# Five tiles instead of six in a weight ring, and the token-major weights 192 bytes into them

## The chip, the cores and the metric

One Trainium2 core runs the whole layer. Its engines work side by side and wait for each other by semaphores: TensorE (PE in the profile; PEld is its weight load), VectorE (DVE), ScalarE (ACT), GpSimd (POOL) and SyncE (SP), which issues all DMAs here. The metric is the device time of one execution in microseconds (us), median of several runs.

## The reference

One decoder layer on 512 tokens of width 1024, all in float32. The parts that matter here are the projections of the normalised input `h` and what hangs on them:

```python
z = h @ w_in                                  # queries, keys, values, gates, pool inputs
q = rope(rms_norm(q, q_norm_w), pos) * SCALE
k = rope(rms_norm(kv[:, :, :, 0], k_norm_w[:, None, :]), pos)
y_pool = pool_mixer(u_pool, pool_w, pool_scale) @ w_pool_br
y_attn = nsa_attention(q, k, v, nsa_g, ...) @ w_attn_br    # compressed, selected, window
merged = merge_g[:, :, 0] * y_pool + merge_g[:, :, 1] * y_attn
x = x + merged @ w_o
x = x + conv_ffn(rms_norm(x, ffn_norm_w), ...)             # 5504 wide, gated
```

## The kernel before

Every float32 operand is held as two parts, `hi` (rounded by ScalarE) and `lo` (the rest, subtracted by VectorE or GpSimd; `split`, L92 to L103), and a product is three matmuls: high by high, low by high, high by low. TensorE is kept fed from one ring of weight buffers in SBUF (`Ring`, L148). A call loads up to 1024 columns into one of two `st` buffers by DMA, and splits them into tiles of 512 columns, tags `hi` and `lo`, six of each. A tile is written again only when every matmul that reads its last content is done.

Two kinds of projection draw on it. Feature-major ones (`fm_tile`, matmul lines L109 to L111) use the weights as the stationary operand and stream 512 tokens; a call's 1024 columns are two tiles of each part, used up one after the other by 12 matmuls each. Token-major ones (`tok_gemm`, L319 to L321; names `tg`) use the input as the stationary operand and stream 256 weight columns; a group is two calls (`tm_weights`), four tiles of each part, and since it goes through all eight slices of the input for each of four token blocks (24 matmuls a block), it holds all four tiles until its last block. There are six such groups, two for keys and values (`kv_group`) and four for queries (`q_group`), 6 x 4 x 24 = 576 matmuls.

After a token block comes a chain: ScalarE scales and squares (L293, L294), VectorE sums (L296), ScalarE takes the root (L297), VectorE and GpSimd rotate (L300 to L303), VectorE multiplies (L308, L311), TensorE transposes (`kt`, L350; `qt`, L371), and ScalarE and VectorE write keys and queries (L97/L100, L376/L377). Beside them run the pool inputs (`pool_in`, whose `lo` parts GpSimd makes), the pool's mixing (`pool_mix`, names `pl`, `plo`, L103) and the compression (`cmp_in`, `cmp_hid`, names `ct`, `hp`, L473). PSUM has two banks for `fm`, `pl` and `hp` together.

A scheduler of the language sets each engine's order when the program is built: it puts the instructions of the source in an order by its own estimate of when each can start, and knows of the tiles. So a tile fewer changes the order, too. After the projections comes attention with gate projections filled in between (`fill`), then the output projection and the feed-forward part, all fed by the same ring.

Of the kernel before, what the change touches and what calls it, by code (L numbers as in the profile page):

```python
# [12 lines left out]
F32R = mybir.dt.float32r  # L13
# [6 lines left out]
P = 128  # L20
# [40 lines left out]
TW = (0,) * 6  # L61
# [15 lines left out]
def layer(ctx: ExitStack, tc: tile.TileContext, par, masks, xT, w_kva, w_tm, w_fm, w_pl, w_pbr,  # L77
# [5 lines left out]
    def nm(s):  # L83
        cnt[0] += 1
        return f"{s}{cnt[0]}"
# [31 lines left out]
    wr = pool(ctx, "wr")  # L117
# [30 lines left out]
    class Ring:  # L148
        def __init__(self, p, half, bufs):
            self.p, self.half, self.bufs = p, half, bufs  # L150

        def __call__(self, src, w, n, eng=None, cast=None):

            st = self.p.tile([P, 1024], F32, tag="st", name=nm("st"), bufs=self.bufs[0])
            nc.sync.dma_start(st[:, :n * w], src)
            out = []
            per = self.half // w
            for i in range(0, n, per):
                m = min(per, n - i)
                hi = self.p.tile([P, self.half], F32R, tag="hi", name=nm("hi"), bufs=self.bufs[1])  # L160
                lo = self.p.tile([P, self.half], F32R, tag="lo", name=nm("lo"), bufs=self.bufs[1])
                split(hi[:, :m * w], lo[:, :m * w], st[:, i * w:(i + m) * w], eng=eng, cast=cast)
                out += [(hi[:, j * w:(j + 1) * w], lo[:, j * w:(j + 1) * w]) for j in range(m)]
            return out

    ring = Ring(wr, 512, (2, 6))


    pk = cp.tile([P, NKEEP], F32, name="pk")
# [152 lines left out]
            yield t, ps  # L322

    def tm_weights(i):
        return ring(w_tm[:, i, :1024], 256, 4, TW[i] and g) + ring(w_tm[:, i, 1024:], 256, 4, TW[i] and g)

    heads = lambda ap: ap.rearrange("p (h d) -> p h d", d=DH)

# [130 lines left out]
    def cmp_hid(i):  # L459
# [3 lines left out]
        for c in range(2):  # L463
            st = wr.tile([P, 1024], F32, tag="st", name=nm("st"), bufs=ring.bufs[0])
            nc.sync.dma_start(st, cw1[i, :, c * 1024:(c + 1) * 1024])
            for p_ in range(4):
                tag = ("hi", "lo")[p_ % 2]
                w = wr.tile([P, 2, 2, P], F32R, tag=tag, name=nm(tag), bufs=ring.bufs[1])
                split(w[:, 0], w[:, 1], st[:, 256 * p_:256 * p_ + 256].rearrange("p (b h) -> p b h", b=2),
                      eng=CW and g)  # L470
                for b in range(2):
                    q_ = 8 * c + 2 * p_ + b
                    pe.matmul(hv, X[:, q_].rearrange("p j g n -> p (j g n)"), w[:, :, b],  # L473
                              start=q_ == 0, stop=q_ == 15)
# [89 lines left out]
    at = ExitStack()  # L564
# [401 lines left out]
```

## Time and profile before

| | us |
|---|---|
| median of 3 runs (843.36 to 844.0) | 843.49 |
| the profiled execution | 842.97 |
| its span, first to last instruction | 840.9 |
| TensorE busy in the span | 817.7 (97%) |
| VectorE busy | 571.4 (68%) |
| ScalarE busy | 464.4 (55%) |
| GpSimd busy | 233.7 (28%) |

The profile is of one execution. Matmuls overlap, so how fast TensorE goes is read from one start to the next, not from the duration of one. The projections fill the span's first 182 us, attention goes to about 480, and the feed-forward part is the rest. TensorE's clock stood at its upper level but for two stretches, one from 107 to 114 us and one from 182 to 186 us.

### The profile page before, as it was taken

The page shows a single profiled execution, that of the slowest core. Times are in us where ns is not written, and L with a number is a line of the kernel's source. Part 1 is how long each engine was busy: PE and PEld are TensorE (multiplying, and loading weights), DVE is VectorE, ACT ScalarE, POOL GpSimd, SP SyncE. Part 2 cuts the span into 40 slices and gives each one's busy share as a digit, 9 for nine tenths or more (in the row PEclk, how much of TensorE's full clock was granted, in tenths as well). Part 3 has the DMA queues.
Part 4 walks back from the last instruction along what each step waited for, and adds up shares of the span by engine and source line. Part 5 has one row for each costly group of instructions (what it writes and reads, how often), then busy time and mean ns, then how long its engine had stood idle before and what let it go on. Part 6 is the DMA issues. An engine that isn't in the chain of part 4 may idle for free.

```text
span 840.9 us, 12107 instructions
## 1 busy us (share of the span) xinstructions
PE 817.7 (97%) x4291; PEld 696.8 (83%) x4291; DVE 571.4 (68%) x1194; ACT 464.4 (55%) x985; POOL 233.7 (28%) x326
## 2 busy tenths in 40 slices
PE   7999989989999999999999999999999999999998
PEld 6888878968878878788888888888888888888888
DVE  7599976778887888886565438877777777522321
ACT  6755767757787877785334436544554454322220
POOL 5696714347575655642001200000000000000000
PEclk9999989999999999999999999999999999999999
DMA  6333132330100101011443332233332333343430
GB/s 217 103 101 113 51 101 96 107 101 25 51 26 26 51 17 35 27 39 42 135 149 112 101 103 77 101 101 101 100 91 90 97 100 116 92 128 103 113 101 26
DMA packets 23116, 72.82 MB, mean 87 GB/s; under 512 B 2832, under 2 KB 3472, under 8 KB 23056
## 3 DMA queue, kind: packets, MB, share of 16 engines
q1 hardware_dynamic: 23056, 72.05, 27.5%
q8 instruction: 34, 0.56, 0.3%
q14 instruction: 26, 0.21, 0.1%
HBM read 69.94 MB, written 2.10 MB: 86 GB/s over the span
## 4 chain that ended last, share of the span: by engine, by line
PE 85%; DVE 7%; ACT 3%; DMA 2%; issue 1%; POOL 0%; SPq 0%; ACTq 0%; DVEq 0%; POOLq 0%
PE fm L109 16%; PE fm L111 16%; PE fm L110 16%; PE op L729 5%; PE dn L109 5%; PE dn L111 5%; PE dn L110 5%; PE tp L722 4%; PE ss L691 2%; PE ss L692 2%; PE tg L321 2%; PE tg L319 2%; PE tg L320 2%; DMA st<-in_w_fm 1%; PE pb L109 1%
## 5 line engine op out<-in xcount | busy, mean ns | idle before, releaser
L97 ACT ACTIVATE hi<-st 128x512 fp32r<-128x512 f32 (+3 forms) x253 | 152.2, 607 | 189.3 <-PE fm L110 89.6
L100 DVE TENSOR_TENSOR lo<-st,hi 128x512 fp32r<-128x512 f32 (+1 forms) x210 | 145.2, 695 | 100.5 <-ACT hi L97 99.2
L109 PE MATMUL fm<-h2h,hi 128*128 128x512 f32 x344 | 134.0, 389 | 0.0
L110 PE MATMUL fm<-h2l,hi 128*128 128x512 f32 x344 | 133.8, 389 | 0.0
L111 PE MATMUL fm<-h2h,lo 128*128 128x512 f32 x344 | 133.7, 389 | 0.0
L703 POOL TENSOR_TENSOR pb<-pb,sm 128x128 f32<-128x128 f32 (+3 forms) x128 | 91.8, 748 | 49.8 <-DVE sm L700 26.1
L681 ACT ACTIVATE pb<-pb,nm 128x384 f32<-128x384 f32 (+3 forms) x128 | 70.9, 555 | 16.2 <-DVE nm L680 15.4
L111 PEld LDWEIGHTS fm<-h2h,lo 128*128 128x128 f32 x344 | 64.6, 188 | 13.5
L110 PEld LDWEIGHTS fm<-h2l,hi 128*128 128x128 f32 x344 | 64.6, 188 | 13.4
L109 PEld LDWEIGHTS fm<-h2h,hi 128*128 128x128 f32 x344 | 64.6, 188 | 13.2
L109 PE MATMUL fm<-hh,hi 128*128 128x512 f32 x160 | 71.7, 448 | 0.0
L680 DVE CUSTOM_DVE_ANT_0 pb<-ss,mk 128x384 f32<-128x384 f32 (+3 forms) x128 | 58.9, 486 | 16.7 <-PE ss L692 13.2
L110 PE MATMUL dn<-gl,hi 128*128 128x512 f32 (+1 forms) x189 | 69.1, 365 | 0.0
L111 PE MATMUL dn<-gh,lo 128*128 128x512 f32 (+1 forms) x189 | 69.1, 365 | 0.0
L109 PE MATMUL dn<-gh,hi 128*128 128x512 f32 (+1 forms) x189 | 69.1, 365 | 0.0
L111 PE MATMUL fm<-hh,lo 128*128 128x512 f32 x160 | 63.4, 397 | 0.7 <-POOL lo L100 0.7
L100 DVE TENSOR_TENSOR ptl<-tp,pth 128x512 fp32r<-128x512 f32 (+1 forms) x96 | 56.6, 594 | 10.8 <-ACT pth L97 10.2
L110 PE MATMUL fm<-hl,hi 128*128 128x512 f32 x160 | 63.4, 396 | 0.0
L97 ACT ACTIVATE pth<-tp 128x512 fp32r<-128x512 f32 (+1 forms) x96 | 49.3, 517 | 22.8 <-PE tp L722 22.5
L100 POOL TENSOR_TENSOR lo<-st,hi 128x512 fp32r<-128x512 f32 x36 | 47.2, 1313 | 41.6 <-ACT hi L97 35.6
L319 PE MATMUL tg<-hi,hh 128*128 128x256 f32 x192 | 54.4, 286 | 0.0
L320 PE MATMUL tg<-hi,hl 128*128 128x256 f32 x192 | 54.4, 286 | 0.0
(256 smaller groups left out, 1815.9 us busy)
## 6 DMA issues: line engine op xcount, KB each, us to landing
st<-in_w_up SPq DMA_DIRECT2D x43, 512.0 KB, 3.5
st<-in_w_dn SPq DMA_DIRECT2D x24, 448.0 KB, 3.4
st<-in_w_fm SPq DMA_DIRECT2D x20, 512.0 KB, 3.5
st<-in_w_tm SPq DMA_DIRECT2D x12, 512.0 KB, 3.4
st<-in_w_ab SPq DMA_DIRECT2D x8, 512.0 KB, 3.5
st<-in_w_o SPq DMA_DIRECT2D x8, 512.0 KB, 3.4
x<-in_xT SPq DMA_DIRECT2D x15, 256.0 KB, 3.7
st<-in_cw SPq DMA_DIRECT2D x4, 512.0 KB, 3.5
```

Source lines behind the costliest of these rows:

```text
L97: a.activation(hi, src, AF.Copy)
L100: (eng or v).tensor_tensor(lo, src, r32(hi), ALU.subtract)
L109: pe.matmul(ps, sh, mh_, start=first and i == 0, stop=False)
L110: pe.matmul(ps, sh, ml_, start=False, stop=False)
L111: pe.matmul(ps, sl, mh_, start=False, stop=last and i == n - 1)
L319: pe.matmul(ps[:, :n], hh[k][:, tt], H, start=k == 0, stop=False)
L320: pe.matmul(ps[:, :n], hl[k][:, tt], H, start=False, stop=False)
L680: v.tensor_tensor_reduce(p_, ps, mcaus[:, S - n:], -1.0, 3e38, ALU.add, ALU.min, nm_[:, i:i + 1])
L681: a.activation(p_, p_, AF.Exp, bias=nm_[:, i:i + 1], scale=-1.0, accum_out=sm[:, i:i + 1])
L703: g.tensor_tensor(pb[:, PBASE[i]:PBASE[i] + n], pb[:, PBASE[i]:PBASE[i] + n], sm[:, i:i + 1].to_broadcast([P, n]), ALU.mult)
L722: last = pe.transpose(tp[:, n:n + P], pb[:, PBASE[i] + j * P:PBASE[i] + (j + 1) * P], ident)
L729: pe.matmul(op[:, j * P:], V2[b][j][:, G], pt_[:, TBASE[j]:TBASE[j] + w], start=b == 0 and j == 0 and part == 0, stop=False)
```

## The change

A ring tile is now 576 columns long (512 and 64 to spare), and there are five for each part instead of six. The token-major projections' weights begin 48 columns (192 bytes) into their tiles; all others begin at the start as before. The tiles of one part lie 2304 bytes apart instead of 2048, and the ring is 1536 bytes shorter, so the buffers allocated behind it move down by that much. No operation is added or removed.

```diff
+        def part(self, tag, at=0):
+            t = self.p.tile([P, self.half + 64], F32R, tag=tag, name=nm(tag), bufs=self.bufs[1])
+            return t[:, at:at + self.half]
+
-        def __call__(self, src, w, n, eng=None, cast=None):
+        def __call__(self, src, w, n, eng=None, cast=None, at=0):
...
-                hi = self.p.tile([P, self.half], F32R, tag="hi", name=nm("hi"), bufs=self.bufs[1])
-                lo = self.p.tile([P, self.half], F32R, tag="lo", name=nm("lo"), bufs=self.bufs[1])
+                hi, lo = self.part("hi", at), self.part("lo", at)
...
-    ring = Ring(wr, 512, (2, 6))
+    ring = Ring(wr, 512, (2, 5))
...
     def tm_weights(i):
-        return ring(w_tm[:, i, :1024], 256, 4, TW[i] and g) + ring(w_tm[:, i, 1024:], 256, 4, TW[i] and g)
+        return (ring(w_tm[:, i, :1024], 256, 4, TW[i] and g, at=48)
+                + ring(w_tm[:, i, 1024:], 256, 4, TW[i] and g, at=48))
...
-                w = wr.tile([P, 2, 2, P], F32R, tag=tag, name=nm(tag), bufs=ring.bufs[1])
+                w = ring.part(tag).rearrange("p (a b h) -> p a b h", a=2, b=2)
```

The order moves on all engines between 25 and 182 us and hardly after. Three places follow. The first is ScalarE's order where the first feature-major weights are split (`hi102`, `hi104`: the two halves of the first pool input's; `hi65`, `hi67`: the last of the first group's). Before:

```order
L97 ACTIVATE hi67_511<-st64_505 128x512
L97 ACTIVATE hi102_709<-st101_707 128x512
L97 ACTIVATE hi104_713<-st101_707 128x512
L197 ACT_TABLE_LOAD
L197 ACTIVATE sr36_364<-nsum35_361,eps_111 128x512
```

In the changed kernel `hi102` stands there alone, and `hi104` comes 25 rows later, in the same one free tile, when the matmuls on `hi102` are done:

```order
L301 ACT_TABLE_LOAD
L301 ACTIVATE hss42_428<-hss42_428,eps_111 128x2
L348 ACTIVATE V202_139<-tg85_611,rstd_117 128x2x64
L297 ACTIVATE h49_459<-raw2_353,rstd_117 128x128
L298 ACTIVATE h50_460<-h49_459 128x128
L301 ACTIVATE hss47_446<-hss47_446,eps_111 128x2
L97 ACTIVATE hi104_713<-st101_707 128x512
```

So the second half of the first pool input's weights has gone from before the table load to behind seven small steps of the key chain; before, those steps ended in `hi111`, the next pool input's.

The second place is TensorE's order after the compression's matmuls (`hp`), at the transposes of the second query group's third and fourth blocks (`qt283`). Before, 24 matmuls of the next query group (`tg342`, `tg350`, `tg357`) stand between the two:

```order
L473 MATMUL hp291_1605<-lo301_1645,X185_1117 128x256 x2
L371 MATMUL qt283_1555<-pk_109,qd277_1539 128x128 x2
L319 MATMUL tg342_1808<-hi333_1790,hh0_120 128x256
L320 MATMUL tg342_1808<-hi333_1790,hl0_128 128x256
L319 MATMUL tg350_1852<-hi333_1790,hh0_120 128x256
L320 MATMUL tg350_1852<-hi333_1790,hl0_128 128x256
```

Now both pairs of transposes follow each other, and the next group's matmuls come after the pool's output (`pb`):

```order
L479 MATMUL hp291_1605<-lo301_1645,X185_1117 128x256 x2
L377 MATMUL qt283_1555<-pk_109,qd277_1539 128x128 x2
L377 MATMUL qt283_1555<-pk_109,qd285_1583 128x128 x2
L457 MATMUL ct306_1664<-pk_109,dup307_1665 128x128
L457 MATMUL ct306_1664<-pk_109,dup308_1668 128x128
L457 MATMUL ct306_1664<-pk_109,dup309_1671 128x128
L486 MATMUL ht303_1654<-pk_109,hs302_1650 128x64
L109 MATMUL pb321_1716<-plo242_1377,hi317_1708 128x512
```

So nothing stands any more between the transposes that need `qd277` and those that need `qd285`.

The third place is VectorE's order around the same stretch, from the second of the pool's mixed parts (`plo244`) to the third (`plo246`), whose PSUM bank `hp` takes over. Before:

```order
L103 SCALAR_TENSOR_TENSOR plo244_1384<-pl243_1380,pk_109,plo244_1384 128x512
L311 TENSOR_TENSOR qd270_1492<-h272_1494,hrs275_1505 128x2x2x64
L100 TENSOR_TENSOR X185_1117<-ct191_1142,X185_1117 64x8x31
L100 TENSOR_TENSOR lo318_1709<-st316_1706,hi317_1708 128x512
L305 RECIPROCAL hrs282_1552<-hss281_1545 128x4
L100 TENSOR_TENSOR lo320_1713<-st316_1706,hi319_1712 128x512
L377 TENSOR_TENSOR qp196_1163<-qt230_1317,qp196_1163 64x2x256
L311 TENSOR_TENSOR qd277_1539<-h279_1541,hrs282_1552 128x2x2x64
L103 SCALAR_TENSOR_TENSOR plo246_1391<-pl245_1387,pk_109,plo246_1391 128x512
```

Now, with the two `lo` behind it:

```order
L103 SCALAR_TENSOR_TENSOR plo244_1384<-pl243_1380,pk_109,plo244_1384 128x512
L309 RECIPROCAL hrs282_1552<-hss281_1545 128x4
L315 TENSOR_TENSOR qd277_1539<-h279_1541,hrs282_1552 128x2x2x64
L383 TENSOR_TENSOR qp196_1163<-qt230_1317,qp196_1163 64x2x256
L300 TENSOR_REDUCE hss289_1589<-h287_1585 128x4
L103 SCALAR_TENSOR_TENSOR plo246_1391<-pl245_1387,pk_109,plo246_1391 128x512
```

Seven instructions stood between the two, and four do now; `qd285` comes 13 instructions after `plo246` in the changed order and 12 after it before, and among the 13 are a different choice of `lo` parts and two steps of the compression.

## Rows read from the trace of the kernel before

**Rows 1.** Page, the chain that ended last: share of the span by engine.

```profile
PE 85%; DVE 7%; ACT 3%; DMA 2%; issue 1%; POOL 0%; SPq 0%; ACTq 0%; DVEq 0%; POOLq 0%
```

**Rows 2.** Busy time by stretch; after the engines, granted clock, DMA share, GB/s.

```profile
22.00:60.00 38.00, 36.39 (x212) 31.47 (x212) 26.51 (x62) 23.85 (x60) 28.67 (x51) 1.00 0.35 108
60.00:85.00 25.00, 23.20 (x184) 22.21 (x182) 24.17 (x53) 13.30 (x37) 17.71 (x29) 1.00 0.32 99
85.00:107.00 22.00, 18.99 (x149) 17.63 (x147) 20.82 (x47) 18.20 (x47) 16.42 (x28) 1.00 0.23 72
107.00:114.00 7.00, 5.55 (x26) 5.55 (x27) 6.75 (x14) 4.98 (x11) 0.15 (x1) 0.51 0.34 90
520.00:665.00 145.00, 145.00 (x642) 120.05 (x641) 111.57 (x168) 74.68 (x112) 0.00 (x0) 1.00 0.31 98
```

**Rows 3.** Timeline of TensorE: start, us, instruction, count; the pace of 256-column matmuls.

```profile
27.27 0.28 PE L319 MATMUL tg<-hi,hh 128*128 128x256 f32 x1
...
27.99 0.28 PE L319 MATMUL tg<-hi,hh 128*128 128x256 f32 x1
...
150.04 0.41 PE L473 MATMUL hp<-hi,X 128*128 128x256 f32 x2
...
151.97 0.28 PE L319 MATMUL tg<-hi,hh 128*128 128x256 f32 x1
```

**Rows 4.** Timeline, 27 to 41 us: splitting the pool inputs' weights.

```profile
26.93 1.15 ACT L97 ACTIVATE hi<-st 128x512 fp32r<-128x512 f32 x2 [1.39 <-DMA st<-in_w_fm]
...
34.41 0.47 PE L109 MATMUL fm<-hh,hi 128*128 128x512 f32 x1
...
38.80 0.61 ACT L97 ACTIVATE hi<-st 128x512 fp32r<-128x512 f32 x1
...
39.32 0.47 ACT L297 ACTIVATE hss<-hss,eps 128x2 f32<-128x2 f32 x2
...
39.55 1.28 POOL L100 TENSOR_TENSOR lo<-st,hi 128x512 fp32r<-128x512 f32 x1 [4.80 <-PE fm L111]
...
39.80 0.40 PE L110 MATMUL fm<-hl,hi 128*128 128x512 f32 x1
...
40.88 0.50 PE L111 MATMUL fm<-hh,lo 128*128 128x512 f32 x1 [0.68 <-POOL lo L100]
```

**Rows 5.** Timeline, 103 to 115 us: the hole before the compression, and what follows it.

```profile
103.46 0.74 DVE L103 SCALAR_TENSOR_TENSOR plo<-pl,pk,plo 128x512 fp32r<-128x512 f32 x1
...
107.65 0.74 DVE L103 SCALAR_TENSOR_TENSOR plo<-pl,pk,plo 128x512 fp32r<-128x512 f32 x1
...
108.45 0.79 PE L473 MATMUL hp<-hi,X 128*128 128x256 f32 x2 [3.24 <-DVE plo L103]
...
109.04 0.63 PE L473 MATMUL hp<-lo,X 128*128 128x256 f32 x2
...
109.47 0.63 PE L473 MATMUL hp<-hi,X 128*128 128x256 f32 x2
...
113.16 0.56 PE L319 MATMUL tg<-hi,hh 128*128 128x256 f32 x1
...
113.61 0.69 DVE L100 TENSOR_TENSOR lo<-st,hi 128x512 fp32r<-128x512 f32 x1
...
114.22 0.42 DVE L311 TENSOR_TENSOR qd<-h,hrs 128x256 f32<-128x256 f32 x1
```

**Rows 6.** Timeline at 182 us: the first compressed scores' transposes.

```profile
181.89 0.90 PE L629 MATMUL scq<-pk,cst 128*128 128x128 f32 x4 [3.39 <-DVE cst L624]
```

**Rows 7.** Timeline: one kind of VectorE step, alone and beside a GpSimd addition.

```profile
41.44 0.27 DVE L303 TENSOR_TENSOR h<-h,h 128x128 f32<-128x128 f32 x1
...
44.49 1.03 POOL L402 TENSOR_TENSOR pa<-pu 128x511 f32<-128x511 f32 x1
44.59 1.08 DVE L303 TENSOR_TENSOR h<-h,h 128x128 f32<-128x128 f32 x1
```

**Rows 8.** Waits, 186 to 841 us: us in total, times, longest.

```profile
ACT hi L97 <- PE fm L110: 88.8, 74, 4.1
```

## The prediction

> **What bounds the kernel now.** I read the chain that ended last first. TensorE holds 85% of it, VectorE 7%, ScalarE 3% and DMA 2% [rows 1]: what counts is time in which TensorE stands still or goes slowly. Then busy time by stretch [rows 2]. From 520 to 665 us TensorE is busy for 145.00 of 145 us with 642 matmuls, 145/642 = 0.226 us for each of 512 columns. The projections are another matter: 36.39 of 38 us from 22 to 60, 23.20 of 25 us from 60 to 85, 18.99 of 22 us from 85 to 107, and 5.55 of 7 us from 107 to 114, there at a granted clock of 0.51, the lower level (1.2 GHz). VectorE is busy for 24.17 + 20.82 + 6.75 = 51.7 of the 54 us from 60 to 114, so what is pushed back on VectorE there stays pushed back. The DMA share is at most 0.35. Last came the timelines of the places where the order moves [rows 4 to 6], and the waits of the rest [rows 8].
>
> So the change can act in four ways: by the address, by the tiles of the attention and feed-forward parts, by the order in the projections, and by the clock.
>
> **The address.** The 576 token-major matmuls read the same 256 columns 192 bytes further on. Between two that stand six apart, start to start is (27.99 - 27.27)/6 = 0.120 us; the compression's matmuls, which have another moving operand at another address, follow at (151.97 - 150.04)/16 = 0.121 us [rows 3]. By columns, 256/512 of 0.226 is 0.113 us; what does not shrink with the columns is twice the difference, 0.014 us. The pace is the same for two tensors that lie apart, so I take 0 for the shift. The bounds are that it takes away the whole fixed part, 576 x 0.014 = 8 us, or adds as much.
>
> The Trainium skill ("TensorE: Matmul & The Clock Gate", section "Wait — 56ns, not 53.3ns?") has a matmul take N/2.4 GHz and about 2.5 ns more when warm, 109 ns for 256 columns, and names no address; if the 120 ns of the row were brought to that, an estimate of (0.120 - 0.109) x 576 = 6.3 us would be gained, and no run here shows it.
>
> **Five tiles after 182 us.** ScalarE's `hi` waits there 74 times for TensorE, 88.8 us in all, 4.1 us at the longest [rows 8]: the splits are ahead of the matmuls and wait for tiles to come free. One tile fewer makes them wait longer, and TensorE, busy throughout [rows 2], does not see it as long as a split in one free tile (0.61 us for `hi` [rows 4]) fits into the 12 x 0.226 = 2.7 us of the tile before. I take 0; bounds 0 and +2.
>
> **The order, first place (34 to 42 us).** A token-major group holds four of five tiles through its four blocks, so one is left for feature-major halves: `hi104` can only be written when the matmuls on `hi102` are done. Before, `hi102` and `hi104` are split together, two in 1.15 us at 26.93 [rows 4], and all 24 matmuls run without a stop. In the changed order only the first 12 do. They start at 34.41 [rows 4], two token-major ones later, at 34.65, and TensorE is through at 34.65 + 2.71 = 37.4. ScalarE then has `hi104` where the next input's `hi` stood, which ran at 38.80 for 0.61 us [rows 4], with about 0.2 for one more `hss` ahead of it (two took 0.47): it ends at about 39.6, and TensorE waits 2.2 us. GpSimd's `lo` takes 1.28 us [rows 4] and ends at 40.9; TensorE has two matmuls, 0.46 us, in between and waits 0.85 more. Against these 3.1 us goes the stop of before, 39.80 + 0.23 to 40.88 [rows 4], 0.85 us, as the next input's `lo` is now covered by 24 token-major matmuls. The sum is +2.3 us; bounds +0.5 (if ScalarE's table loads fall luckily) and +4.
>
> **Second place (42 to 104 us).** The keys' transposes now stand after only four matmuls of the next input and wait for the last key step behind VectorE, and the second mixed part has some three more VectorE steps ahead, of 0.3 to 0.42 us each (`qd` took 0.42 [rows 5]), 1.0 to 1.4 us. VectorE has 45.0 us of work in the 47 from 60 to 107 [rows 2], so most of a push there arrives at TensorE. I take +1.5 us; bounds 0 and +3.4.
>
> **Third place (103 to 115 us).** Before, the compression's matmuls wait for `plo246`, 3.24 us, as the granted clock falls [rows 2, 5]. From one `plo` to the next VectorE needs 4.19 us [rows 5] with seven steps in between; with four, the wait shrinks to about 1.4 us. But the work behind it is as long as it was: `qd285` comes 13 steps after `plo246` rather than 12, and ended at 114.22 + 0.42 = 114.64 [rows 5]. Before, TensorE had 24 x 0.12 = 2.9 us of token-major matmuls from 113.16 on [rows 5] to cover that; now its transposes stand next, and TensorE waits. It gets through the two pairs at about 114.64 + 0.3 = 114.9, less 0.3 to 0.4 for the shorter `lo` work among the 13, 114.5, having done what was done at 113.16 and one pair (0.2) more: +1.2 us. What the hole gives back is thus lost at the transposes. Bounds: -0.7 (if the steps ahead of `qd285` move up with the hole) and +3.5 (if none of it does and two more steps get in).
>
> **Fourth (182 us).** The scores wait 3.39 us for `cst` [rows 6], which has one score step directly ahead on VectorE in both orders. 0, bounds -1.4 and +1.4.
>
> **Clock.** The compression's matmuls from 108.45 to 109.04 and 109.47 go at (109.47 - 109.04)/2 = 0.215 us instead of 0.12 [rows 3, 5]; 16 such cost 16 x 0.095 = 1.5 us, and the rest of the stretch somewhat more. A shorter hole might leave the clock up; the new waits at 37 to 41 us might bring it down once. I take 0, bounds -2.8 and +3.4 (one more such stretch).
>
> **Sum.** 2.3 + 1.5 + 1.2 + 0 = +5.0 us. On the profiled execution's 842.97 us that makes 848.0; the median of the runs is 843.49, half a microsecond above, well inside the range.
>
> **Rivals.**
>
> *Contention, dearer.* A VectorE addition of two SBUF operands took 0.27 us by itself and 1.08 beside a GpSimd addition [rows 7], 0.81 more. The changed order moves the key chain's steps against GpSimd's `lo` and pooling steps. If three of that chain fall beside them, 3 x 0.81 = 2.4 us come on top, and if the holes then bring one more stretch at the lower clock, 1.5 to 3.4 more: 852 to 855. For it: VectorE's lack of slack. Against: GpSimd is busy beside VectorE in before as well, so steps may as well move out of its way.
>
> The Trainium skill ("SBUF — State Buffer", section "Who interferes with whom") says that a VectorE instruction with two SBUF inputs contends with a GpSimd one that reads SBUF, and here the trace agrees, 1.08 against 0.27 us [rows 7].
>
> *Covered.* The new waits only take the place of old ones: TensorE stands idle for 38 - 36.39 = 1.6, 1.8, 3.0 and 1.5 us in the stretches of [rows 2], and if it now waits for tiles where it waited for VectorE and GpSimd before, the end moves by less than 1.7 us: 843. For it: the wait for `cst` at 182 us [rows 6] can take up what is lost before it, if VectorE, not TensorE, brings the end of the projections. Against: VectorE's chains hang on TensorE's products as well.
>
> *Not slower: the shorter hole wins.* The hole before the compression falls from 3.24 us to 1.4, -1.8 us; the clock stays up there, -1.5 for the 16 matmuls and -0.4 for transposes beside them; and only half of the first place's +2.3 arrives. Together -2.5: 840.4. It decides if the second pair of transposes waits for less than about 1 us.
>
> *The address.* If the shift spares the fixed part of 0.014 us in each of 576 matmuls, 8 us, of which 3 remain after the order's +5: 840; if it adds as much, 856.
>
> **How the numbers follow.** The forecast, order with new waits in the projections, 848.0 us: 0.60; its own range from the terms, whose bounds won't all come at one end, 845 to 851.5. Contention: 0.14. Covered: 0.12. The shorter hole: 0.09. The address: 0.05. About 0.2% (1.7 us) is what a measurement of this kernel can tell from no change. Faster by more than that takes the shorter hole and half of the address case, with a small part taken off: 0.10. Within it: covered, and the lower edge of the forecast: 0.15. Slower: the rest, 0.75. For 8 in 10 the range is 843.5 to 855: at the low end it leaves out the shorter hole, the gain by address and some of "covered", at the high end hardly more than the address's loss.
>
> **What the next profile would show.** First place right: in the first pool input, a wait of about 2.2 us of the feature-major L109 matmul for `hi` at 37 to 40 us, and 0.9 for `lo`; wrong: 24 matmuls without a stop. Second: a wait of the keys' transposes longer than before, and `plo244` 1 us or more later than the rest. Third: a wait of the compression for `plo246` near 1.4 us, and one of 2 to 3.5 us at the second pair of `qt` transposes. Address: token-major matmuls at 0.120 us from start to start, with the FFN at 0.226. From the scores' first transposes (181.89 us before) to the end, the same time as before within half a microsecond. Any stretch of granted clock at 0.5 other than the two of before is the clock term. The prediction fails if the projections end within 1.7 us of where they did, or if the time after them changes by more than that.

## The result, and the profile after

The changed kernel takes 853.74 us (median of 4 runs, 853.06 to 854.5), the kernel before 843.42 (4 runs) beside it: a ratio of 1.0121 with a 95% interval of 1.0104 to 1.0139, 10.3 us more. Forecast were 848.0 us, +5.0: the direction and the range held, the size did not.

The chain that ended last holds less of TensorE than before [rows 1]:

```profile
PE 79%; DVE 9%; ACT 5%; DMA 5%; issue 2%; POOL 1%; SPq 0%; DVEq 0%; ACTq 0%; POOLq 0%
```

Busy time by stretch, with the columns of [rows 2]; the granted clock is the third number from the end:

```profile
40.00:47.00 7.00, 6.34 (x20) 4.94 (x19) 5.70 (x17) 3.00 (x10) 5.30 (x13) 0.52 0.25 78
...
112.00:115.00 3.00, 2.58 (x6) 1.49 (x6) 2.83 (x7) 1.91 (x5) 1.79 (x4) 0.50 0.54 141
115.00:122.00 7.00, 3.13 (x21) 2.54 (x22) 6.81 (x15) 4.71 (x11) 0.15 (x1) 0.99 0.37 117
122.00:125.00 3.00, 3.00 (x9) 2.16 (x10) 2.24 (x6) 2.31 (x4) 0.76 (x3) 0.50 0.49 171
...
190.50:196.50 6.00, 5.65 (x18) 4.78 (x19) 4.09 (x13) 2.65 (x9) 0.00 (x0) 0.50 0.00 0
520.00:665.00 145.00, 145.00 (x642) 120.05 (x641) 112.67 (x170) 77.27 (x116) 0.00 (x0) 1.00 0.30 97
```

The feed-forward part is the same to the matmul. But four stretches run at the lower clock (1.2 GHz) where there were two. The mean clock of the two profiled executions says the same: 0.988 over 851.1 us is 2 x 0.012 x 851.1 = 20.4 us at half speed, 0.994 over the 840.9 of before 10.1 us. TensorE is busy nearly all through these stretches.

The first place, TensorE from 34 us, answers to [rows 4]:

```profile
34.14 0.39 PE L109 MATMUL fm<-hh,hi 128*128 128x512 f32 x1
...
36.63 0.39 PE L111 MATMUL fm<-hh,lo 128*128 128x512 f32 x1
39.52 0.50 PE L109 MATMUL fm<-hh,hi 128*128 128x512 f32 x1 [2.50 <-ACT hi L97]
39.86 0.57 PE L110 MATMUL fm<-hl,hi 128*128 128x512 f32 x1
41.10 0.79 PE L111 MATMUL fm<-hh,lo 128*128 128x512 f32 x1 [0.66 <-POOL lo L100]
...
42.97 0.63 PE L109 MATMUL fm<-hh,hi 128*128 128x512 f32 x1
43.40 0.63 PE L110 MATMUL fm<-hl,hi 128*128 128x512 f32 x1
```

The two waits are there, 2.50 and 0.66 us where 2.2 and 0.85 were forecast. What follows them was not: the next matmuls start 0.43 us apart (42.97 to 43.40), at half the pace of 0.226.

The third place, TensorE from 105 to 124 us, answers to [rows 5]. Before, the first four of these query transposes and the pairs behind them stood here:

```profile
101.72 0.63 PE L371 MATMUL qt<-pk,qd 128*128 128x128 f32 x4 [0.28 <-DVE qp L377]
...
110.32 1.05 PE L371 MATMUL qt<-pk,qd 128*128 128x128 f32 x4
```

Now:

```profile
106.43 0.28 PE L325 MATMUL tg<-lo,hh 128*128 128x256 f32 x1
108.16 0.63 PE L377 MATMUL qt<-pk,qd 128*128 128x128 f32 x4 [1.46 <-DVE X L100]
109.80 0.41 PE L377 MATMUL qt<-pk,qd 128*128 128x128 f32 x2 [1.01 <-DVE qp L383]
...
111.65 0.80 PE L109 MATMUL pl<-pli,plw 128*128 128x512 f32 x1 [0.68 <-DVE plo L103]
...
115.03 0.48 PE L479 MATMUL hp<-hi,X 128*128 128x256 f32 x2 [0.45 <-DVE plo L103]
...
118.40 0.41 PE L377 MATMUL qt<-pk,qd 128*128 128x128 f32 x2 [1.24 <-DVE qp L383]
121.04 0.44 PE L377 MATMUL qt<-pk,qd 128*128 128x128 f32 x2 [2.23 <-DVE qd L315]
...
122.95 0.79 PE L109 MATMUL pb<-plo,hi 128*128 128x512 f32 x1
123.54 0.63 PE L110 MATMUL pb<-plo,hi 128*128 128x512 f32 x1
123.97 0.63 PE L111 MATMUL pb<-plo,lo 128*128 128x512 f32 x1
```

The hole ahead of the compression shrank from 3.24 us to 0.45 (1.4 was forecast), and the second pair of transposes waits 2.23 us, within the 2 to 3.5 forecast. New to me are the 1.01 us ahead of the transposes at 109.80: they stood amid the compression's matmuls before (110.32) and now stand ahead of the pool's last mixing. The first four wait 1.46 us, where they waited 0.28. VectorE is busy for 6.81 of the 7 us from 115 to 122. And the `pb` matmuls behind start 0.43 us apart again.

At the scores the wait is about as long as in [rows 6] (3.16 against 3.39 us), but 8.96 us later, and the lower clock sets in there for 6 us and more:

```profile
190.85 1.11 PE L635 MATMUL scq<-pk,cst 128*128 128x128 f32 x4 [3.16 <-DVE cst L630]
```

Up to the first four query transposes, and up to the scores' transposes, both traces hold the same number of matmuls of each name. So the loss can be read there: +6.4 us at the first (108.16 against 101.72), +9.0 at the second, +10.2 at the end of the span. What stands behind the scores' transposes, which I had said would take the same time within half a microsecond, takes 1.2 us longer.

The token-major matmuls, which had 0.120 us from start to start [rows 3], are quicker. In two stretches of six they have (24.86 - 24.18)/6 = 0.113 and (26.72 - 26.01)/6 = 0.118 us:

```profile
24.18 0.28 PE L325 MATMUL tg<-lo,hh 128*128 128x256 f32 x1
...
24.86 0.28 PE L325 MATMUL tg<-lo,hh 128*128 128x256 f32 x1
...
26.01 0.28 PE L323 MATMUL tg<-hi,hh 128*128 128x256 f32 x1
...
26.72 0.28 PE L325 MATMUL tg<-lo,hh 128*128 128x256 f32 x1
```

That would be worth about 576 x 0.004 = 2.3 us, and yet the kernel is 10.3 us slower. The experiments have to part three things: the address, the waits of the new order, and the clock behind the waits.

### The profile page after: what moved, and what is told of

Read it like the earlier page. It is cut to its first block, busy times and chain, and to the rows that moved or that the text cites. A ratio compares the mean times of both kernels' runs of the same rounds, so it can differ in the third digit from the quotient of the medians.

```text
span 851.1 us, 12165 instructions
## 1 busy us (share of the span) xinstructions
PE 821.9 (97%) x4291; PEld 698.9 (82%) x4291; DVE 569.5 (67%) x1194; ACT 465.6 (55%) x985; POOL 231.4 (27%) x326
## 4 chain that ended last, share of the span: by engine, by line
PE 79%; DVE 9%; ACT 5%; DMA 5%; issue 2%; POOL 1%; SPq 0%; DVEq 0%; ACTq 0%; POOLq 0%
PE fm L111 16%; PE fm L109 16%; PE fm L110 16%; PE op L735 5%; PE dn L111 5%; PE dn L110 5%; PE dn L109 5%; PE tp L728 4%; PE ss L697 2%; PE ss L698 2%; DMA st<-in_w_fm 2%; DMA st<-in_w_tm 1%; ACT hi L97 1%; DVE lo L100 1%; DMA st<-in_cw 1%
## 5 line engine op out<-in xcount | busy, mean ns | idle before, releaser
L100 DVE TENSOR_TENSOR lo<-st,hi 128x512 fp32r<-128x512 f32 (+1 forms) x210 | 142.5, 683 | 97.4 <-ACT hi L97 96.4
```

Source lines behind the costliest of these rows:

```text
L100: (eng or v).tensor_tensor(lo, src, r32(hi), ALU.subtract)
```

## The experiments

Each kernel ran beside the kernel before on its chip; the medians of before were 843.42 to 844.07 us.

| kernel | us | ratio to before, 95% |
|---|---|---|
| changed | 853.74 | 1.0104 to 1.0139 |
| e1_count, five tiles, no shift | 851.48 | 1.0078 to 1.0111 |
| e5_ladder, six shifts | 854.41 | 1.0096 to 1.0138 |
| e9_64, 64 bytes | 853.19 | 1.0094 to 1.013 |
| e6_first, a pair more for group 1 | 847.12 | 1.0023 to 1.0051 |
| e7_third, a pair more for groups 4, 5 | 853.14 | 1.0096 to 1.0125 |
| e10_pow, five tiles, four `lo` on GpSimd | 852.97 | 1.0088 to 1.0125 |
| e13_fill, changed, stops filled | 848.95 | 1.0044 to 1.0068 |
| e16_fill0, five tiles, stops filled | 849.04 | 1.0051 to 1.0078 |
| e3_ring, before, ring 64 bytes on | 852.26 | 1.0086 to 1.0115 |
| e4_all, before, inputs and ring on | 844.82 | 1.0004 to 1.0023 |
| e8_ffn, one run | 858.19 | |
| e11_bpow1, e12_bpow2, before, `lo` on GpSimd | 843.7, 843.27 | 0.9992 to 1.0009, 0.9987 to 1.0004 |
| e14_bfill, before, stop filled | 844.6 | 0.9997 to 1.0016 |
| e15_both, before, both of these | 844.98 | 1.0002 to 1.0026 |

**Five tiles without the shift** (`e1_count`). The order on every engine is that of the changed kernel.

```diff
-            t = self.p.tile([P, self.half + 64], F32R, tag=tag, ...)
+            t = self.p.tile([P, self.half], F32R, tag=tag, ...)
-        return (ring(w_tm[:, i, :1024], 256, 4, TW[i] and g, at=48) + ...
+        return (ring(w_tm[:, i, :1024], 256, 4, TW[i] and g) + ...
```

> Five tiles of 512 columns, all weights from the start of their tiles: the change without its 192 bytes; the order is that of the changed kernel. Theory A (the shift quickens the token-major matmuls, the tile count costs): start to start of those matmuls goes back from the changed kernel's 113 to 118 ns to 120, 576 x 0.004 = 2.3 us, so 853.7 + 2.3 = 856 us (855 to 857); the lower clock stretches at 40 to 47, 112 to 115, 122 to 125 and 190 to 197 us stay. Rival B (the quicker pace comes of something else that changed, the order or the tiles' distance): pace as in the changed kernel and 853.7 us. Rival C (my forecast's 0 for the shift, all of the time from the order): the same 853.7 at a pace of 120 ns.

851.48 us: none of the three. The pace is 0.120 again, as theory A has it, but the time is lower than the changed kernel's, not higher. The profiled executions differ in the clock, 0.994 here:

```profile
40.00:47.00 7.00, 6.16 (x38) 5.20 (x38) 6.79 (x22) 3.95 (x12) 6.59 (x16) 1.00 0.27 78
111.00:118.00 7.00, 5.99 (x23) 4.76 (x21) 6.74 (x14) 5.45 (x13) 1.65 (x4) 0.52 0.27 87
...
190.00:197.00 7.00, 6.43 (x33) 5.52 (x34) 6.02 (x18) 3.77 (x12) 1.28 (x1) 1.00 0.01 2
```

After nearly the same stop (2.37 and 0.84 us) the clock stayed up this time: 38 matmuls from 40 to 47 us against 20. It is also up at the scores; down it is from 111 to 118 us and from 121 to 124.5, and the two make as much lower clock as the kernel before had. At that equal clock it is still slower by 6.5 us: 850.35 us against 843.86, the median of the 11 runs of before beside it that had 0.994. The first query transposes come at 106.86 us, +5.1 and not +6.4, the scores' at 190.57, +8.7:

```profile
106.86 0.63 PE L377 MATMUL qt<-pk,qd 128*128 128x128 f32 x4 [0.91 <-DVE X L100]
...
190.57 0.66 PE L635 MATMUL scq<-pk,cst 128*128 128x128 f32 x4 [3.02 <-DVE cst L630]
```

Its four runs had clocks of 0.994, 0.990, 0.988 and 0.991 and spans of 848.4, 849.8, 850.6 and 849.2 us. One program, one order: 0.006 of clock is 2.2 us. The changed kernel's four had 0.986 to 0.988. So a part of its loss is the clock, and the larger part, by this run, is not.

**Where the shift's pace comes from** (`e5_ladder`, `e3_ring`, `e4_all`, `e8_ffn`).

```diff
+ e5:  ring(w_tm[:, i, :1024], ..., at=(0, 8, 16, 24, 32, 48)[i])      # changed kernel
+ e3:  wr = pool(ctx, "wr"); wr.tile([P, 16], F32, name="pad")         # kernel before
+ e4:  xp = pool(ctx, "xp"); xp.tile([P, 16], F32, name="pad")         # kernel before
+ e8:  ps = fm2(w_up[t], h2h, h2l, at=8 * (t % 8))                     # five tiles, no shift for tg
+      ws += ring(w_dn[...], P, 7, at=8 * ((3 * c + q_) % 8))
```

> The changed kernel with another start for each of the six token-major groups: 0, 32, 64, 96, 128 and 192 bytes into the tiles (96 matmuls each). The order is that of the changed kernel. Theory A: the pace of a group depends on its start alone; the first group has 120 ns, the last 113 to 118, and where the others lie shows whether the step is of 64, 128 or 256 bytes. The time lies between the changed kernel's 853.7 and 856 us, about 855. Rival B (order or tile distance, not the start): all six at 113 to 118 ns and 853.7 us.

> The kernel before, six tiles and its order, with 64 unused bytes ahead of the ring: the ring's tiles and all buffers behind them begin 64 bytes further on, the normalised inputs (hh, h2h) don't. Theory A1 (the start of the moving operand matters, and 64 bytes do as 192): the token-major matmuls, whose moving operand is in the ring, go from 120 to about 116 ns, and the down projection's, whose moving operand lies behind the ring, get quicker too, while the feed-forward up projections, whose moving operand h2h stays, keep 226.6 ns; 576 x 0.004 + 567 x 0.004 = 4.6 us less, about 839. Rival A2 (the distance between moving and stationary operand matters): token-major and up projections (344 x 3 matmuls) get quicker, the down projection, where both move, does not; 2.3 + 4.1 = 6.4 less, about 837. Rival A3 (64 bytes do nothing): 843.4 with all paces as before.

> The kernel before, six tiles and its order, with 64 unused bytes ahead of the normalised inputs: hh, h2h, the ring and all behind it begin 64 bytes further on, so that moving and stationary operands keep their distance. Theory A1 (start of the moving operand): all 512-column feature-major matmuls, some 2080, get quicker by about 4 ns as well as the 576 token-major ones; 2656 x 0.004 = 10.6 us less, about 833. Rival A2 (distance of the two operands): nothing changes, 843.4. Rival A3 (64 bytes do nothing): 843.4 too, told from A2 by the kernel with the pad ahead of the ring alone.

> Five tiles of 576 columns, token-major weights from the start, and the feed-forward part's weights, which are stationary there, 0, 32, 64, ..., 224 bytes into their tiles, another for each call in turn; the moving operand stays. Theory D (what counts is how far apart the moving and the stationary operand begin, modulo 256 bytes): the pace of a 512-column matmul depends on the call's start; at 0 it is 226.4 ns, at 64 about 233 as in the kernel with 64 bytes ahead of the ring, and some of the other six lie below 226. Rival E (0 is the best for 512 columns): all others lie above, 227 to 236, and the time is 5 to 10 us above that of five tiles. Rival F (only the start of the moving operand counts): all at 226.4.

The pace depends on how far apart moving and stationary operand begin, not on either alone. In the ladder the six groups have medians of 120 ns at 0 bytes, 117 at 32, 116 to 117 at 64, about 120 at 96 and 128, and 117 to 118 at 192. The bytes are not all of it: in the changed kernel, with 192 bytes throughout, the first three groups have 114 ns and the last three 117 to 118, and no run here shows why. With 64 bytes ahead of the ring, the token-major matmuls are quicker (114 to 118) but the 512-column ones of the feed-forward part slower: from 599.77 to 601.88 us nine steps, 0.234 us each, against 0.226:

```profile
599.77 0.40 PE L110 MATMUL fm<-h2l,hi 128*128 128x512 f32 x1
...
601.88 0.39 PE L110 MATMUL fm<-h2l,hi 128*128 128x512 f32 x1
```

From 520 to 665 us it gets through 623 matmuls, where before had 642 [rows 2], and the kernel takes 852.26 us. That is theory A2 by its mechanism and its opposite by its sign: for 512 columns, apart is worse. In `e4_all`, where both move, the pace is back at 0.226 and so, nearly, is the time. The exception is the output projection, whose moving operand lies on the other side of SBUF and stayed: its 192 matmuls need 6 ns more each, 1.2 us, and 844.82 - 843.76 is 1.1. The compression's matmuls, whose moving operand moved with the ring and whose stationary one did not, go from 120 to 118 ns in both kernels. `e8_ffn` closes it for the up projections (theory E): 227 ns in the median with 0 bytes, 229 with 192, and 232 to 237 with the other six; the one run took 858.19 us. So nothing is to be gained there for 512 columns; for 256 columns there is, 2 to 6 ns.

**Does the quicker pace reach the end?** (`e9_64`, the changed kernel with `at=16`.)

> The changed kernel with 64 instead of 192 bytes. The token-major matmuls keep the quicker pace (113 to 118 ns), by the distances measured so far. Theory G (a quicker token-major pace gains nothing at the end, because TensorE then waits the longer for ScalarE and VectorE, and the longer stops bring the clock down more often): 853.7 us, granted clock 0.986 to 0.990 in all runs, like the changed kernel. Rival H (the changed kernel's 2.3 us above five tiles of 512 come from its other addresses or by chance of the runs): 851.5 or less, with clocks of 0.988 to 0.994 as with five tiles of 512.

853.19 us, with clocks of 0.988, 0.994, 0.988, 0.988 and 0.989: theory G by the time and four of the five clocks, while the run at 0.994 lies outside it. That run says more than the others: its span was 848.6 us, that of `e1_count` at 0.994 848.4. At equal clock the quicker pace gives nothing, as far as one run of each can show, and the kernel is 7.2 us above the runs of before at 0.994 (850.73 against 843.49).

**Mending one place at a time** (`e6_first`, `e7_third`): five tiles of 512, no shift, and one more pair of tiles, which only some groups may use.

```diff
+                hi, lo = (self.part(p + "x" * (x and not i)) for p in ("hi", "lo"))   # bufs=1
+        return (ring(w_tm[:, i, :1024], 256, 4, TW[i] and g, x=i in (0,))             # e7: (3, 4)
```

> Five tiles of 512 columns and one more pair that only the first token-major group may use: during that group two tiles of each part are free for feature-major halves, as before, and TensorE's order up to the third pool input is that of the kernel before. Theory A (the cost of a tile fewer falls at separate places, each with its own waits): the first two places, where TensorE had lost 4.5 us more by 106 us than before with five tiles of 512 (851.5 us), are mended, the third stays: about 847 us (846 to 848.5). Rival B (VectorE sets the end of the projections, so what is won early is lost again at the transposes after 106 us): 850.5 to 852. Rival C (it is the lower clock alone): no lower clock at 40 to 47 us in any run, and 849.5.

> Five tiles of 512 columns and one more pair that only the fourth and fifth token-major groups may use. The order up to 85 us is that of five tiles; after it the transposes qt268 stand amid the compression's matmuls again, as before, and no more ahead of the pool's mixing, while the pairs of qt283 still follow each other. Theory A (separate places): of the 3.7 us that TensorE loses more than before from 101 to 122 us with five tiles, what the waits at qt268 take (1.2, 0.5 and part of 0.8 us) goes, but the compression's wait for plo246 comes back in part; 849.5 us (848.5 to 850.5). Rival B (VectorE's chain alone decides, whatever TensorE has in between): 851.5. Rival C (all of the third place goes): 847.8.

`e6_first` is theory A on the number: 847.1. TensorE is busy for 12.29 of the 13 us from 34 to 47, at the full clock:

```profile
34.00:47.00 13.00, 12.29 (x69) 10.17 (x68) 10.38 (x29) 8.98 (x24) 7.51 (x15) 1.00 0.14 47
```

So the first two places cost 4.4 us without the shift (851.5 to 847.1), and what is won there is not lost again later. What is left is 3.1 us (847.12 against 843.98 beside it). `e7_third` is a miss, 853.1, above all three theories: the `qt268` transposes no longer wait ahead of the pool's mixing, but the compression again waits 3.28 us for `plo246` and the second `qt283` pair 2.13 for `qd285`:

```profile
115.08 0.51 PE L479 MATMUL hp<-hi,X 128*128 128x256 f32 x2 [3.28 <-DVE plo L103]
121.51 0.44 PE L377 MATMUL qt<-pk,qd 128*128 128x128 f32 x2 [2.13 <-DVE qd L315]
```

In this order, too, TensorE waits there for what VectorE brings, which is rival B's mechanism; why the time is 1.6 us above rival B's 851.5 stays open. That no order of TensorE's would mend the third place isn't shown: one was tried.

**Taking work from VectorE there** (`e10_pow` on five tiles; `e11_bpow1`, `e12_bpow2` on the kernel before).

```diff
-POW = (0,) * 4
+POW = (1, 1, 0, 0)     # e10, e12; e11: (1, 0, 0, 0)
```

> Five tiles of 512 columns as in the first experiment, and the lo parts of the first two pool output weights (lo318 to lo327, four of 128x512) made by GpSimd instead of VectorE. TensorE's order at the third place stays; VectorE has 7 instead of 13 steps from plo246 to qd285. Theory A (the third place costs because VectorE, busy without a stop from 105 to 123 us, brings qd285 late and TensorE has no token-major matmuls left to cover it): four steps of about 0.62 us less, so the wait of the second qt283 pair, 2.1 us there, falls under 0.3, and of the 3.7 us lost more than before about 1.5 are left: 851.5 - 2.2 = 849.3 us (848.3 to 850.3). Rival B (it is the ring: the matmuls behind wait for tiles): the wait moves from the transposes to pb321 or tg342, 851 to 852. Rival C (GpSimd, 1.3 us a step, holds up pb321): 851.5 or more.

> The kernel before (six tiles) with the lo parts of the first pool output weights (lo318, lo320) made by GpSimd; TensorE's order is that of before, VectorE has two steps of 0.6 to 0.7 us less between plo244 and plo246. Theory A (the compression's wait of 3.4 us hangs on VectorE): the wait shrinks by 1.3 us to about 2.1, and the time is 843.8 - 1.3 = 842.5 us; if the clock stays up there more often, 841.5. Rival B (what is won there is waited for later, at the scores' transposes at 182 us or at qt283): 843.8.

> The kernel before (six tiles) with the lo parts of the first two pool output weights (four) made by GpSimd. Theory A: as with two, 842.5, and nothing more at the second qt283 pair, which did not wait before; the third pair of lo steps and what hangs on it comes earlier by 1.2 us on VectorE, so the qt283 pairs and the next query group may gain up to 0.5. Rival B: 843.8. Rival C (GpSimd's four steps of 1.3 us hold up the pool's outputs): 844.5 or more.

None is faster beyond its interval. Four `lo` steps left VectorE, and others got slower: in `e10_pow` a multiplication that takes 0.41 to 0.43 us elsewhere took 1.37 beside GpSimd's `lo`, and `qd` 1.30:

```profile
113.59 1.37 DVE L306 TENSOR_TENSOR h<-h,C 128x256 f32<-128x256 f32 x1
...
117.64 1.30 DVE L315 TENSOR_TENSOR qd<-h,hrs 128x256 f32<-128x256 f32 x1
```

```profile
113.40 1.28 POOL L100 TENSOR_TENSOR lo<-st,hi 128x512 fp32r<-128x512 f32 x1 [0.81 <-ACT hi L97]
...
117.40 2.67 POOL L100 TENSOR_TENSOR lo<-st,hi 128x512 fp32r<-128x512 f32 x2
```

In `e12_bpow2` a `qd` of 0.42 us took 1.54, and the compression's wait stayed at 3.41 us. This is the mechanism of my contention rival [rows 7]. The Trainium skill ("SBUF — State Buffer", section "Who interferes with whom") says that a VectorE instruction with two SBUF inputs contends with a GpSimd one that reads SBUF; the trace agrees, 1.37 against 0.42 us. Theory A of `e10_pow` isn't shown by it: the wait of the second `qt283` pair fell from 1.86 us in `e1_count` to 1.05, and the first pair now waits 1.58.

**Keeping the clock up** (`e13_fill`, `e16_fill0`, `e14_bfill`): matmuls whose result nobody reads, in the stops.

```diff
+    def fill(n, mv):
+        for _ in range(n):
+            pe.matmul(FB[:, :256], hh[0][:, :P], mv, start=True, stop=True)
...
+        mm3(ps, ...ws[:4]..., last=False); fill(n, V2[0][1]...)   # 18, first pool input alone
...
+            if gq == 1 and t > 1: fill3((5, 8)[t - 2])            # 13 of 512 columns on plh[3]
...
+ e14:  hv = ...; fill(9 * (i == 0), plh[2])                      # kernel before: 9 of 512 columns
```

> The changed kernel with 31 matmuls more whose results nobody reads: 18 of 256 columns (2.1 us) in the stop between the two halves of the first pool input's matmuls, 13 of 512 columns (2.9 us) after the compression's matmuls, ahead of the two pairs of qt283 transposes. VectorE's and ScalarE's work is the same; some 30 matmuls stand a little elsewhere in TensorE's order. Theory K (the lower clock that follows the stops at 37 to 41 and 117 to 121 us costs 2.1 and 1.7 us): the stretches of lower clock at 40 to 47 and 121 to 125 us are gone, the granted clock of a run is 0.992 or more, and the time is 853.7 - 2.1 - 1.7, of which 1 is taken back by VectorE's waits behind: 851 us (850 to 852). Rival L (the stops themselves are the cost, what the clock takes is waited for anyway): the clock as in theory K, but 853 to 854.5. Rival M (the extra matmuls delay the rest): above 854.5.

> Five tiles of 512 columns, all weights from the start of their tiles, with the 31 unused matmuls in the same two stops; the order is that of the changed kernel with the 31. Theory N (the quicker token-major pace is taken back by waits for VectorE and ScalarE, and the changed kernel was slower than five tiles of 512 by its clock alone): 848.9 us like the changed kernel with the 31, within 0.7, clock 0.992 to 0.994. Rival O (the pace counts): 848.9 + 2.3 = 851.2. Rival P (the shift costs by itself): 848 or less.

> The kernel before with nine matmuls of 512 columns more (2.0 us), whose results nobody reads, in the stop of 3.4 us ahead of the compression's matmuls. Theory K: the stretch of lower clock at 107 to 114 us is gone in most runs, clock 0.996 to 0.998, and the time is that of the kernel before in its runs with 0.998: 842.3 (1.2 us below 843.5). Rival L: the clock as in theory K, the time 843.5. Rival M (the extra matmuls delay the compression): above 844.2. Should nine not be enough to keep the clock up, the clock stays at 0.994 and the time at 843.5, and the run says nothing on the price.

With 31 more matmuls the changed kernel is 4.8 us faster, 848.95. TensorE in the first stop and the stretches after both:

```profile
37.35 2.31 PE L319 MATMUL fb<-V,hh 128*128 128x256 f32 x18
39.89 0.50 PE L109 MATMUL fm<-hh,hi 128*128 128x512 f32 x1 [0.23 <-ACT hi L97]
40.23 0.40 PE L110 MATMUL fm<-hl,hi 128*128 128x512 f32 x1
41.46 0.50 PE L111 MATMUL fm<-hh,lo 128*128 128x512 f32 x1 [0.83 <-POOL lo L100]
```

```profile
40.00:47.00 7.00, 6.17 (x38) 5.27 (x39) 6.70 (x22) 4.43 (x13) 6.21 (x14) 1.00 0.25 76
109.00:116.00 7.00, 5.75 (x19) 4.39 (x20) 6.77 (x14) 5.87 (x15) 3.32 (x5) 0.53 0.48 150
117.00:125.00 8.00, 7.88 (x42) 6.29 (x41) 6.97 (x18) 3.59 (x8) 1.22 (x5) 1.00 0.41 133
188.00:191.50 3.50, 3.50 (x12) 3.05 (x13) 2.71 (x9) 1.42 (x6) 0.00 (x0) 0.52 0.00 0
```

The second half still starts at 39.89 us: the stop is as long as it was, for ScalarE's `hi`. But the matmuls from 40 to 47 and from 117 to 125 us now go at the full clock, and the stretch at the scores is 3.5 us and not 6; the one from 109 to 116 us is longer than in the changed kernel. All five runs had clocks of 0.992 to 0.994, that of the kernel before. It gained more than theory K's 2.7. But the order moved as well: some 30 other matmuls, some 30 steps of VectorE and 20 of ScalarE stand elsewhere, most of them between 124 and 153 us. So the 4.8 us are not the clock's alone. The two points of equal work tell where they come from:

```profile
106.80 0.63 PE L382 MATMUL qt<-pk,qd 128*128 128x128 f32 x4 [1.49 <-DVE X L100]
...
187.97 1.12 PE L645 MATMUL scq<-pk,cst 128*128 128x128 f32 x4 [3.51 <-DVE cst L640]
```

| later than before by, us | first query transposes | scores' transposes | end of the span |
|---|---|---|---|
| changed | 6.4 | 9.0 | 10.2 |
| `e1_count`, clock up at 40 to 47 us without filling | 5.1 | 8.7 | 7.5 |
| `e13_fill`, clock up there by filling | 5.1 | 6.1 | 6.1 |

Up to the first query transposes, the lower clock costs 1.3 us, and it makes no difference whether it stays up with filled stops or without. Between the two points the filled kernel loses 1.0 us and `e1_count` 3.5; there the clock (121 to 124.5 us in `e1_count`) and the other order come together, and nothing run here parts them. Behind the scores' transposes the filled kernel needs the time of the kernel before, the changed one 1.2 us more and `e1_count`, without a lower clock there, 1.2 less.

`e16_fill0` is the same without the shift: 849.04 us, theory N. With the clock kept up, the shift is worth nothing, to 0.7 us. Where its pace goes can be read at the waits: TensorE waits 1.02 us at the keys' transposes at 76 us with the shift and 0.69 without, 1.49 and 0.95 at the first query transposes, 3.51 and 2.82 at the scores. It comes earlier to the same late operand.

In the kernel before, nine matmuls did keep the clock up from 107 to 114 us:

```profile
107.00:114.00 7.00, 5.51 (x36) 4.36 (x34) 6.75 (x14) 4.83 (x12) 0.22 (x2) 1.00 0.32 93
```

They brought nothing in the median (844.6 us against 844.07 beside it): TensorE got to the next query group sooner and waited 1.5 us there for a `lo` of VectorE. Beside the kernel before that is rival L, but the runs, parted by their clock, show two things that cancel. Two runs at 1.000 took 842.74 and 843.12 us, two at 0.994 took 846.22 and 846.32, where 14 runs of before at 0.994 have a median of 844.3. So the nine matmuls, with the order that they bring, cost about 2 us at equal clock (rival M), and the clock gives as much back (theory K). `e15_both` joined them with the four `lo` on GpSimd:

> The kernel before with nine unused matmuls of 512 columns in the stop ahead of the compression's matmuls, and the lo parts of the first two pool output weights made by GpSimd. With the nine alone the clock stayed up, but TensorE waited 1.7 us for lo334 behind VectorE; with the four lo alone nothing changed. Theory Q (VectorE's lo steps hold up the query group there): the wait for lo334 goes, and the time is 844.3 - 1.5 = 842.8 us. Rival R (VectorE's steps get slower beside GpSimd's, 0.4 to 1.3 us each, and the wait stays): 844.3.

844.98 us, rival R: `lo334` is no longer waited for, but the second `qt283` pair waits 1.60 us behind a `qd` that took 1.30 us beside GpSimd. No kernel of these beats the one before.

## Why the prediction was wrong

- **The address, 0 (bounds -8 and +8).** The pace did change, 0.120 to 0.113 to 0.118, so the reason I gave (the same pace for two tensors that lie apart) was wrong. The compression's matmuls and the token-major ones draw their moving operand from the same ring, and what differs between them is the stationary one. That both pairs lay at the same distance modulo 256 bytes fits `e4_all`, where the compression's pair moved apart and went from 120 to 118 ns; no trace has the addresses. As a term of the sum 0 was right: 848.95 against 849.04 us with the clock kept up. The 109 ns that follow from the Trainium skill ("TensorE: Matmul & The Clock Gate", section "Wait — 56ns, not 53.3ns?"), which I had set beside the row, were not reached.
- **Five tiles after 182 us, 0.** Right: the feed-forward part is the same to the matmul.
- **First place, +2.3.** Right in mechanism and size: waits of 2.50 and 0.66, less the 0.68 of [rows 4], are +2.5.
- **First two places, 2.3 + 1.5 = 3.8.** 4.4 by `e6_first`, without the shift. Up to the first query transposes it is 5.1 with the clock up.
- **Third place, +1.2.** The hole fell further than I said (0.45 rather than 1.4), the second pair waits 2.23, in the 2 to 3.5 forecast; missed was that the earlier transposes moved, too, and wait 1.01 us of their own. With the first two places mended (`e6_first`), 2.1 us are left at equal clock (845.6 us, its one run at 0.994, against 843.49).
- **The clock, 0 (bounds -2.8 and +3.4).** This is the step that failed. I had one new stretch at 37 to 41 us as the upper bound, and took the middle, without a row that spoke for it. There are new stretches at 40 to 47 and 122 to 125 us, and the one at the scores grew from about 3.5 to over 6 us; against these, the one of 107 to 114 us shrank to 112 to 115. In all, 20.4 us at the lower level stand against 10.1.

What the 10 us more of lower clock cost can be bounded in two ways. At equal clock (0.994) five tiles without the shift are 6.5 us above the kernel before (`e1_count`), so of the changed kernel's 10.3 us the clock has about 3.8. Filling the stops brought the 10.3 us above the kernel before beside it down to 4.9, which is 5.4; but `e16_fill0`, at 0.994, is only 4.6 us above before where `e1_count` is 6.5, so about 1.9 of the 5.4 come with the other order, and 3.5 are left for the clock. Both rest on `e1_count`'s single run at 0.994, and two runs of one kernel at one clock can lie 1.5 us apart (`e6_first` at 0.990: 845.7 and 847.17), so these sizes hold to a microsecond or two. So the sum went wrong like this: the clock, forecast at 0, came to some 3.5 to 4 us, and the waits, forecast at 5.0, to about 6.5 (4.4 + 2.1). That the filled kernel ends at +4.9, almost the +5.0 forecast, is luck: its stops are as long as the changed kernel's, and its order is another.

It would be wrong to price a stretch at half of what TensorE is busy in it. For 0.006 of the mean clock that would be 5.1 us (2 x 0.006 x 845, halved). Runs of one program, parted by their clock, show less; that the rest goes into waits which come anyway is likely, but not shown:

| kernel | at the lower clock, us | at the higher clock, us | difference |
|---|---|---|---|
| before, beside `e1_count` | 843.86 (0.994, 11 runs) | 841.84 (0.998, 3 runs) | 2.0 for 0.004 |
| `e1_count` | 852.57 (0.988, 1 run) | 850.35 (0.994, 1 run) | 2.2 for 0.006 |
| `e14_bfill` | 846.27 (0.994, 2 runs) | 842.93 (1.000, 2 runs) | 3.3 for 0.006 |
| `e15_both` | 846.92 (0.994, 2 runs) | 842.75 (1.000, 3 runs) | 4.2 for 0.006 |

In `e6_first` no price shows at all: 845.7 and 847.17 us at 0.990, 845.6 at 0.994.

The clock was not an independent risk with two signs. It hung on the other terms: I had put two stops of 2 to 3 us each in front of long runs of matmuls, and the row of before that shows what can follow stood in front of me [rows 2], a stop of 3.24 us with a clock of 0.51 beside it.

The Trainium skill ("Perfetto Trace Analysis", section "Matmul Optimizations") puts it in one line, "it's important that matmuls execute back-to-back in batches". The trace agrees: with the two stops filled, the granted clock is 1.00 behind them where it was 0.52 and 0.50. It does not follow each time: after nearly the same stop at 37 to 41 us the clock fell in the changed kernel's profile and not in `e1_count`'s. What decides it there is open.

Of the rivals, the contention added nothing: slow steps stand in both profiles, as a `kd` step of 1.40 us at 50.16 us in the kernel before and one of 1.39 at 49.22 us in the changed one, where it takes 0.41 alone. "Covered" was wrong. The shorter hole did come, but the second pair waited well over the 1 us that I had named as the point of decision.

## What to carry to other kernels

A new stop on TensorE can be priced twice: the wait, and then what the matmuls behind it lose at the lower clock, which is up to half of their busy time, and in four programs here was 2.0 to 4.2 us for what could have been 3.4 to 5.1. Where a sum of waits puts stops like these (2.50 and 2.23 us) ahead of dense matmuls, the second price belongs in the sum, not only in the range. Runs of one program that differ in their clock give that price, and comparing at equal clock keeps it apart from the waits. A matmul that got quicker in stretches where VectorE brings the operands gained nothing here; ask what the engine does with the time before counting it. And before work is moved from VectorE to GpSimd, look at which VectorE steps will run beside it.

## What the runs showed of the hardware that was not expected

- The pace of these fp32 matmuls depends on how far apart the moving and the stationary operand begin. For 512 columns in the feed-forward part, 227 ns where both begin as in the kernel before and 229 to 237 with the weights 32 to 224 bytes on; for 256 columns, 120 ns as before and 113 to 118 with 64 or 192 bytes between them. A pad of 64 bytes in the wrong place cost 8.5 us (852.26 against 843.76).
- 31 matmuls that compute nothing made a kernel 4.8 us faster (848.95 against 853.74), together with the change of order that they brought.
- In one program the lower clock differs from run to run: five tiles without the shift, 0.988 to 0.994 and 850.6 to 848.4 us of span. A stop of 2.50 us was followed by the lower clock, one of 2.37 us in the same place and order was not.
